# Gate and up by seven products of halves: two of four weight sums of a block moved from VectorE to accumulating DMAs

## Chip, cores and metric

One Trainium2 chip, one core. The metric is device time in microseconds (us) of one execution; lower is better. A chip of its own ran the kernel before three times; differences of about one per cent, 6 us, can be told from none.

## The reference, cut to what matters

A two-layer decoder trunk on 256 tokens of width 1024 in float32. Layer 0 mixes tokens with gated linear attention, layer 1 with block attention; each mixer is followed by a residual layer norm, a SwiGLU FFN of 2816 hidden columns, and another residual layer norm. The change lies in the FFN:

```python
def swiglu_ffn(x, w_gu, w_down):
    gate, up = jnp.split(x @ w_gu, 2, axis=-1)
    return (jax.nn.silu(gate) * up) @ w_down
...
for i in range(DEPTH):
    ...
    x = layer_norm(DEEPNORM_ALPHA * x + y, ln_g[i, 0], ln_b[i, 0])
    x = layer_norm(DEEPNORM_ALPHA * x + swiglu_ffn(x, ffn_w_gu[i], ffn_w_down[i]), ln_g[i, 1], ln_b[i, 1])
```

## The kernel before

**Precision.** Every float32 operand of a matmul is split into a high and a low part (float32r): ScalarE casts the high part (L513 for the units below), VectorE subtracts it from the raw tile to get the low part (L514). A product is then three matmuls on TensorE: high x high, low x high, high x low (`mm3`, L289 to L291; in the blocks below L536, L538, L539).

**The FFN.** `ffn` (L456) first makes 512 of the 2816 columns in the ordinary way (`act_block`), then 2048 columns in four blocks of 512 (`seven`, L523), then the last 256 (tiles g8, u8). In a block the weights of gate and up are seen as four quarters: two halves of the 1024 input rows (kh = 0, 1) by gate and up (gu = 0, 1). A quarter is loaded as two units of 128 x 1024 floats, 512 KB each (`load_unit`, L506, issued on SP's DMA queue). The block's 2 x 2 product of halves (two token halves by two input halves, against the quarters) is done in seven products in place of eight, in the manner of Strassen and Winograd. The left sides are halves of x and four sums of them, made once a layer (`x_sums`, s1 to s4). The right sides are three quarters as they are and four sums of quarters. Each product is 12 matmuls of 128 x 128 by 512 columns, accumulated in the PSUM tiles pa, pb, pc. In program order, with the letter that the trace gives the split units:

- A: quarter (0,0), loaded into the two tiles called A.
- B: A + (0,1), summed in place of A by VectorE (`add_to`, L554 to L556); (0,1) is one of the X tiles.
- C: (1,0), another X pair.
- D: A + (1,1), in place of A, by VectorE.
- E: (1,1), an X pair.
- F: (1,1) + (0,1), in place of the (1,1) pair, by VectorE (L586).
- G: A + (1,0), in place of A, by VectorE (L591).

So a block has eight sums of 128 x 1024 on VectorE (four sums of two units), all recorded at L556, and 14 splits. Silu of gate, the multiplication by up, two sets of transposes (tr, L304) and their split follow; the down projection (fy) of the block before is spread over the block, four rows of w_down at a time (`down_now`, each row loaded and split as d0, d1, ...).

**The order.** Nothing is issued in program order. `Plan` (L64) takes every step with a duration that is written by hand for each engine (`pe`, `act`, `dve`, `gps`, `dma`, L230 to L250) and places the steps one by one, the earliest start first, with 41 SBUF tiles of 128 x 1024 floats (S), two of x (T) and eight PSUM banks to share out. Its result is the order of each engine's queue; on the chip each queue runs in that order and waits on semaphores. `pe` plans columns / 2400 + 0.01 us. `dma_add` (L247) plans a DMA that accumulates, issued on GpSimd's queue: 1.3 us of GpSimd and 4.0 us more until it has landed; the kernel before doesn't call it. GpSimd does little else: some sets of zeros and ones, products of the first mixer, and the small powers of the norms.

The lines that make and use the last two sums:

```python
add_to(r4, 0, 1)
product(pa, "s3", [split_unit(f"F{q}", r4[q]) for q in range(2)], False, False)
...
down_now(pend[2:])
add_to(ch, 1, 0)
product(pa, "a11", [split_unit(f"G{q}", ch[q]) for q in range(2)], False, True)
```

Of the kernel before, what the change touches and what calls it, by code (L numbers as in the profile page):

```python
# [12 lines left out]
ALU = mybir.AluOpType  # L13
# [176 lines left out]
def kernel(ctx, tc, x, positions, gla_w_in, gla_w_gk, gla_b_gk, gla_norm_g, gla_w_out,  # L190
                      moba_w_in, moba_w_out, ffn_w_gu, ffn_w_down, ln_g, ln_b,
                      c_f32, c_i32, out):
    nc = tc.nc
# [16 lines left out]
    pl = Plan(slots)  # L210
# [31 lines left out]
        return pl.op("POOL", 0.2 + 0.0022 * n, fn, reads, writes, **kw)  # L242

    def pe(cols, fn, reads, writes, **kw):
        return pl.op("PE", cols / 2400.0 + 0.01, fn, reads, writes, **kw)

    def dma_add(fn, reads, writes, **kw):  # L247
        return pl.op("POOL", 1.3, fn, reads, writes, extra=4.0, **kw)


    def split(name, parts, zero=False):
# [79 lines left out]
    def Tk(T, t, k):  # L331
        return [(T, ("h", t, k // 4)), (T, ("l", t, k // 4))]
# [64 lines left out]
    def feat_block(banks, T, ws):  # L397
        for i, (wh, wl) in enumerate(ws):
            for hp in range(2):
                def f(i=i, wh=wh, wl=wl, hp=hp):  # L400
                    wv = [w.r.rearrange("p (j c) -> p j c", j=2) for w in (wh, wl)]
                    for hh in range(2):
                        ps = banks[hp].f[:, hh * S:(hh + 1) * S].rearrange("p (t c) -> p t c", t=2)
                        for j in range(2):
                            k = 2 * i + j
                            cs = slice((2 * hp + hh) * P, (2 * hp + hh + 1) * P)
                            mm3(ps, wv[0][:, j, cs], wv[1][:, j, cs], T.ap[0][:, :, k, :], T.ap[1][:, :, k, :],
                                k == 0 and hh == 0, k == KT - 1 and hh == 1)
                pe(12 * 256, f, Tk(T, 0, 2 * i) + Tk(T, 1, 2 * i) + [wh, wl], [banks[hp]])

    def v_block(blk, t, T, ws, vt):
        ps = pl.buf("acc", f"v{blk}{t}")
# [43 lines left out]
    def ffn(i, xs, T, gb, dstT, last, x32):  # L456
# [42 lines left out]
        def unit(kh, gu, q, c0):  # L499
            k0 = 4 * kh + 2 * q  # L500
            return wgu[k0 * P:(k0 + 2) * P, HID * gu + c0:HID * gu + c0 + 512].rearrange("(k p) c -> p k c", p=P)

        def uv(b):
            return b.f.rearrange("p (k c) -> p k c", k=2)

        def load_unit(name, src):  # L506
            raw = S_(name)
            dma(lambda: nc.sync.dma_start(uv(raw), src), 512, [], [raw])
            return raw
# [13 lines left out]
        def seven(b, c0, pend):  # L523


            pa, pc, pb = pl.buf("ps", "pa"), pl.buf("ps", "pc"), pl.buf("ps", "pb")
            e1, e2 = S_("e1"), S_("e2")

            def product(ps, left, ws, first, last_):
                st, rd = lhs(left)  # L530
                for q, (wh, wl) in enumerate(ws):
                    def f(q=q, wh=wh, wl=wl):
                        for j in range(2):
                            sh, sl_ = st(2 * q + j)
                            cs = slice(512 * j, 512 * j + 512)
                            nc.tensor.matmul(ps.f, sh, wh.r[:, cs], start=first and q == 0 and j == 0, stop=False,  # L536
                                             skip_group_check=True)
                            nc.tensor.matmul(ps.f, sl_, wh.r[:, cs], start=False, stop=False, skip_group_check=True)  # L538
                            nc.tensor.matmul(ps.f, sh, wl.r[:, cs], start=False, stop=last_ and q == 1 and j == 1,  # L539
                                             skip_group_check=True)  # L540
                    pe(6 * 512, f, rd + [wh, wl], [ps])

            def keep_(ps, dst, j):
                sl = slice(512 * j, 512 * j + 512)
                act(512, lambda: nc.scalar.copy(dst.f[:, sl], ps.f), [ps], [(dst, j)])  # L545

            have = {}

            def get(kh, gu):
                if (kh, gu) not in have:  # L550
                    have[kh, gu] = [load_unit(f"X{q}", unit(kh, gu, q, c0)) for q in range(2)]
                return have[kh, gu]

            def add_to(raws, kh, gu):  # L554
                for q, other in enumerate(get(kh, gu)):
                    dve(1024, lambda q=q, other=other: nc.vector.tensor_tensor(  # L556
                        out=raws[q].f, in0=raws[q].f, in1=other.f, op=ALU.add), [raws[q], other], [raws[q]])

            ch = [load_unit(f"A{q}", unit(0, 0, q, c0)) for q in range(2)]
            product(pa, "a00", [split_unit(f"A{q}", ch[q]) for q in range(2)], True, False)  # L560
            keep_(pa, e1, 0)
            add_to(ch, 0, 1)
            product(pc, "s1", [split_unit(f"B{q}", ch[q]) for q in range(2)], True, False)
            keep_(pc, e2, 0)
            r3 = get(1, 0)
            product(pb, "a01", [split_unit(f"C{q}", r3[q]) for q in range(2)], True, True)
            dve(512, lambda: nc.vector.tensor_tensor(out=e1.f[:, 0:512], in0=pb.f, in1=e1.f[:, 0:512], op=ALU.add),
                [pb, (e1, 0)], [(e1, 0)])
            act(512, lambda: nc.scalar.activation(e1.f[:, 0:512], e1.f[:, 0:512], AF.Silu), [(e1, 0)], [(e1, 0)],
                table="silu")  # L570
            add_to(ch, 1, 1)
            product(pa, "s2", [split_unit(f"D{q}", ch[q]) for q in range(2)], False, False)
            keep_(pa, e1, 1)
            r4 = get(1, 1)
            down_now(pend[:2])
            product(pc, "s4", [split_unit(f"E{q}", r4[q]) for q in range(2)], False, True)
            h, l = S_(f"hT{b}h", True), S_(f"hT{b}l", True)

            def dst(i, cs):
                return (h, l)[i].r.rearrange("p (k c) -> p k c", k=4)[:, :, cs]  # L580
            dve(512, lambda: nc.vector.tensor_tensor(out=e1.f[:, 512:1024], in0=pc.f, in1=e1.f[:, 512:1024],  # L581
                                                     op=ALU.subtract), [pc, (e1, 1)], [(e1, 1)])
            dve(512, lambda: nc.vector.tensor_tensor(out=e1.f[:, 0:512], in0=e1.f[:, 0:512], in1=e1.f[:, 512:1024],
                                                     op=ALU.mult), [(e1, 0), (e1, 1)], [(e1, 0)])
            transpose_split(e1, (h, l), 0, 0, skey=0, dkey=0, dstf=lambda i: dst(i, slice(0, P)))
            add_to(r4, 0, 1)  # L586
            product(pa, "s3", [split_unit(f"F{q}", r4[q]) for q in range(2)], False, False)
            dve(512, lambda: nc.vector.tensor_tensor(out=e2.f[:, 0:512], in0=e2.f[:, 0:512], in1=pa.f,
                                                     op=ALU.subtract), [pa, (e2, 0)], [(e2, 0)])
            down_now(pend[2:])  # L590
            add_to(ch, 1, 0)  # L591
            product(pa, "a11", [split_unit(f"G{q}", ch[q]) for q in range(2)], False, True)
            act(512, lambda: nc.scalar.activation(e2.f[:, 512:1024], pa.f, AF.Silu), [pa], [(e2, 1)], table="silu")  # L593
            dve(512, lambda: nc.vector.tensor_tensor(out=e2.f[:, 512:1024], in0=e2.f[:, 512:1024], in1=e2.f[:, 0:512],  # L594
                                                     op=ALU.mult), [(e2, 0), (e2, 1)], [(e2, 1)])
            transpose_split(e2, (h, l), 1, 1, skey=1, dkey=1, dstf=lambda i: dst(i, slice(P, 2 * P)))
            return [(c0 // P + j, (h, l), lambda j=j: (hv(h)[:, j, :], hv(l)[:, j, :])) for j in range(4)]
# [3 lines left out]
        for b in (8,):  # L601
            c0 = 512 + 256 * b
# [4 lines left out]
            for q in range(2):  # L607
                for c in range(2):
                    for gi, w2 in ((0, g2), (1, u2)):
                        def f(c=c, q=q, gi=gi, w2=w2, pss=pss):  # L610
                            ps = pss[c].f[:, gi * S:(gi + 1) * S].rearrange("p (t c) -> p t c", t=2)
                            cc = slice(c * P, (c + 1) * P)
                            wv = [w.r.rearrange("p (j c) -> p j c", j=4) for w in w2[q]]
                            for j in range(4):
                                k = 4 * q + j
                                mm3(ps, wv[0][:, j, cc], wv[1][:, j, cc], T.ap[0][:, :, k, :], T.ap[1][:, :, k, :],
                                    k == 0 and gi == 0, k == KT - 1 and gi == 1)
                        pe(12 * 256, f, Tk(T, 0, 4 * q) + Tk(T, 1, 4 * q) + list(w2[q]), [pss[c]])
            for c in range(2):
                ps, sil = pss[c], S_("sil")  # L620
                act(256, lambda ps=ps, sil=sil: nc.scalar.activation(sil.f[:, 0:S], ps.f[:, 0:S], AF.Silu),
# [473 lines left out]
```

## Time and profile before

| | us |
|---|---|
| median of 3 runs | 604.07 (600.82 to 606.42) |
| the profiled execution | 606.1, its span 604.3 |
| TensorE matmuls busy | 580.7 (96% of the span) |
| TensorE weight loads busy | 489.9 (81%) |
| VectorE busy | 525.5 (87%) |
| ScalarE busy | 339.6 (56%) |
| GpSimd busy | 22.2 (4%) |
| 16 DMA engines, mean busy share | 55.5%, 110.02 MB moved |

The times of a profile are those of one profiled execution; its span runs from the first to the last instruction. PE is TensorE's matmuls, PEld its weight loads, which run beside the matmuls; DVE is VectorE, ACT ScalarE, POOL GpSimd, SPq the DMA issues of SyncE. Matmuls are pipelined and their ends are modelled, so a busy TensorE can still be waiting. PEclk is the clock granted to TensorE as a share of full speed: 1.00 is 2.4 GHz, 0.50 is 1.2 GHz. The DMA share is the mean busy share of the 16 DMA engines. "out<-in" names what an instruction writes and reads, in the program's names without buffer numbers.

### The profile page before, as it was taken

Reading aid. Unit: us, or ns where it says so; the run is one execution under the profiler, and the core shown is the slowest. Engines: PE = TensorE matmul, PEld = TensorE weight load, DVE = VectorE, ACT = ScalarE, POOL = GpSimd, SP = SyncE. Lnnn points to the kernel's source line nnn. Section 1 sums busy time; section 2 is a strip of 40 time slices with the busy share of each in tenths; the row PEclk is TensorE's granted clock in tenths of the full one; section 3 lists DMA queues with packets and bytes.
Section 4 is the critical chain, followed back from the end, with each engine's and each line's share of the span. In section 5 each row is a group of like instructions: output and inputs, shape, how many; then the busy total and the mean of one; then the engine's idle time right before and its main releaser. Section 6 shows DMA issues by size and latency. Waiting matters only on the chain.

```text
span 604.3 us, 7959 instructions
## 1 busy us (share of the span) xinstructions
PE 580.7 (96%) x3006; PEld 489.9 (81%) x3006; DVE 525.5 (87%) x643; ACT 339.6 (56%) x452; POOL 22.2 (4%) x27
## 2 busy tenths in 40 slices
PE   8999998999999989899999999999999998998995
PEld 7899886888888668589889999888888885867883
DVE  5888369899999998989898688989999999899956
ACT  4893365357675665676264365735676655567510
POOL 1020210100000000000000000000000000000001
PEclk9999999999999989999999999999999998999998
DMA  8984284544838446476557446535475563836301
GB/s 276 378 280 146 98 284 137 181 142 146 295 113 268 136 146 217 146 264 214 170 178 235 146 149 211 164 85 194 143 244 206 173 237 113 253 116 208 121 0 69
DMA packets 51879, 110.02 MB, mean 182 GB/s; under 512 B 4689, under 2 KB 9329, under 8 KB 51842
## 3 DMA queue, kind: packets, MB, share of 16 engines
q1 hardware_dynamic: 51842, 109.53, 55.5%
q8 instruction: 23, 0.38, 0.3%
q14 instruction: 14, 0.11, 0.1%
HBM read 108.47 MB, written 1.05 MB: 181 GB/s over the span
## 4 chain that ended last, share of the span: by engine, by line
PE 87%; DVE 7%; ACT 2%; DMA 2%; issue 1%; SPq 0%; DVEq 0%
PE fy L289 7%; PE fy L291 7%; PE fy L290 7%; PE pa L539 5%; PE pa L538 5%; PE pa L536 5%; PE v L291 2%; PE v L289 2%; PE v L290 2%; PE tr L304 2%; PE y L291 2%; PE y L289 2%; PE y L290 2%; PE pc L536 2%; PE pc L539 2%; PE pc L538 2%
## 5 line engine op out<-in xcount | busy, mean ns | idle before, releaser
L556 DVE TENSOR_TENSOR A<-A,X 128x1024 f32<-128x1024 f32 x48 | 57.3, 1219 | 0.0
L313 ACT CAST xT<-tr 128x512 fp32r<-128x512 f32 x16 | 9.2, 593 | 40.6 <-PE tr L304 40.4
L360 POOL TENSOR_TENSOR st<-st,mhalf 128x1 f32<-128x1 f32 x8 | 7.5, 944 | 496.3 <-DVE st L358 496.3
L545 ACT COPY e<-pa 128x512 f32<-128x512 f32 x16 | 9.4, 587 | 17.5 <-PE pa L539 17.4
L556 DVE TENSOR_TENSOR X<-X,X 128x1024 f32<-128x1024 f32 x16 | 18.8, 1219 | 0.0
L317 DVE TENSOR_TENSOR xT<-tr,xT 128x512 fp32r<-128x512 f32 x16 | 10.7, 687 | 7.2 <-ACT xT L313 4.6
L513 ACT CAST C0h<-X 128x1024 fp32r<-128x1024 f32 x8 | 8.4, 1050 | 15.0 <-DMA X<-in_ffn_w_gu 15.0
L348 DVE SCALAR_TENSOR_TENSOR r<-xn,fy 128x512 f32<-128x512 f32 x8 | 5.5, 684 | 8.4 <-PE fy L291 8.4
L304 PE MATMUL tr<-ident,e 128*128 128x128 f32 x64 | 9.8, 276 | 3.0 <-DVE e L594 3.0
L304 PEld LDWEIGHTS tr<-ident,e 128*128 128x128 f32 x64 | 7.6, 140 | 6.0 <-DVE e L594 4.7
L352 DVE BATCH_NORM_STATS2 st<-r 128x6 f32<-128x512 f32 x16 | 11.1, 693 | 0.5
L513 ACT CAST G1h<-A 128x1024 fp32r<-128x1024 f32 x8 | 8.4, 1050 | 5.3 <-DVE A L556 5.1
L539 PE MATMUL pa<-D0l,s2hl 128*128 128x512 f32 x16 | 7.3, 455 | 4.2 <-DVE D0l L514 4.2
L370 DVE SCALAR_TENSOR_TENSOR xn<-r,st,lnb 128x512 f32<-128x512 f32 x16 | 11.3, 746 | 0.0
L366 DVE SCALAR_TENSOR_TENSOR r<-r,st,lng 128x512 f32<-128x512 f32 x16 | 11.2, 745 | 0.0
L513 ACT CAST A0h<-A 128x1024 fp32r<-128x1024 f32 x8 | 8.4, 1051 | 5.0 <-DMA A<-in_ffn_w_gu 5.0
L513 ACT CAST F0h<-X 128x1024 fp32r<-128x1024 f32 x8 | 8.4, 1054 | 4.5 <-DVE X L556 4.5
L581 DVE TENSOR_TENSOR e<-pc,e 128x512 f32<-128x512 f32 x8 | 5.5, 691 | 6.2 <-PE pc L539 6.2
L513 ACT CAST C1h<-X 128x1024 fp32r<-128x1024 f32 x8 | 8.4, 1052 | 4.1 <-DMA X<-in_ffn_w_gu 4.1
L513 ACT CAST D0h<-A 128x1024 fp32r<-128x1024 f32 x8 | 8.4, 1048 | 4.1 <-DVE A L556 4.1
L513 ACT CAST G0h<-A 128x1024 fp32r<-128x1024 f32 x8 | 8.4, 1053 | 3.8 <-DVE A L556 3.8
L593 ACT ACTIVATE e<-pa 128x512 f32<-128x512 f32 x8 | 4.8, 595 | 9.3 <-PE pa L539 9.3
(1096 smaller groups left out, 2288.9 us busy)
## 6 DMA issues: line engine op xcount, KB each, us to landing
X<-in_ffn_w_gu SPq DMA_DIRECT2D x48, 512.0 KB, 4.9
A<-in_ffn_w_gu SPq DMA_DIRECT2D x16, 512.0 KB, 3.9
lng<-in_ln_g SPq DMA_DIRECT2D x4, 512.0 KB, 3.6
lnb<-in_ln_b SPq DMA_DIRECT2D x4, 512.0 KB, 5.5
x<-in_x SPq DMA_DIRECT2D x4, 256.0 KB, 4.2
d0r<-in_ffn_w_down SPq DMA_DIRECT2D x2, 512.0 KB, 4.5
d1r<-in_ffn_w_down SPq DMA_DIRECT2D x2, 512.0 KB, 4.9
d2r<-in_ffn_w_down SPq DMA_DIRECT2D x2, 512.0 KB, 3.2
```

Source lines behind the costliest of these rows:

```text
L289: nc.tensor.matmul(ps, lh, rh, start=start, stop=False)
L290: nc.tensor.matmul(ps, ll, rh, start=False, stop=False)
L291: nc.tensor.matmul(ps, lh, rl, start=False, stop=stop)
L304: nc.tensor.transpose(ps.f[:, j * P:(j + 1) * P], src.f[:, k * P:(k + 1) * P], ident.f)
L352: nc.vector.bn_stats(st.f[:, 6 * hf:6 * hf + 6], r.f[:, sl])
L366: nc.vector.scalar_tensor_tensor(out=r.f[:, sl], in0=r.f[:, sl], scalar=st.f[:, 12:13], in1=g.f[:, sl], op0=ALU.subtract, op1=ALU.mult)
L370: nc.vector.scalar_tensor_tensor(out=xn.f[:, sl], in0=r.f[:, sl], scalar=st.f[:, 15:16], in1=b.f[:, sl], op0=ALU.mult, op1=ALU.add)
L513: act(1024, lambda: nc.scalar.copy(hi.r, raw.f), [raw], [hi])
L536: nc.tensor.matmul(ps.f, sh, wh.r[:, cs], start=first and q == 0 and j == 0, stop=False, skip_group_check=True)
L538: nc.tensor.matmul(ps.f, sl_, wh.r[:, cs], start=False, stop=False, skip_group_check=True)
L539: nc.tensor.matmul(ps.f, sh, wl.r[:, cs], start=False, stop=last_ and q == 1 and j == 1, skip_group_check=True)
L556: dve(1024, lambda q=q, other=other: nc.vector.tensor_tensor(out=raws[q].f, in0=raws[q].f, in1=other.f, op=ALU.add), [raws[q], other], [ra ...
```

## The change

VectorE makes only the sums for B and D. The sum for F is now made in the pair (0,1): two DMAs on GpSimd's queue (`add_dma`) read (1,1) from HBM and add it onto the tiles, after the sum for B has read them. The sum for G is made in A: two such DMAs read (1,0) from HBM and add it onto A, after D's split has read A. The three products and all else of a block stay. Three of the planner's numbers change with it: a matmul is planned by columns / 2250, twelve matmuls of 256 columns count as 270 columns each, and an accumulating DMA lands 8.0 us after its issue in place of 4.0.

```diff
     def pe(cols, fn, reads, writes, **kw):
-        return pl.op("PE", cols / 2400.0 + 0.01, fn, reads, writes, **kw)
+        return pl.op("PE", cols / 2250.0 + 0.01, fn, reads, writes, **kw)
 
     def dma_add(fn, reads, writes, **kw):
-        return pl.op("POOL", 1.3, fn, reads, writes, extra=4.0, **kw)
+        return pl.op("POOL", 1.3, fn, reads, writes, extra=8.0, **kw)
...
-                pe(12 * 256, f, Tk(T, 0, 2 * i) + Tk(T, 1, 2 * i) + [wh, wl], [banks[hp]])
+                pe(12 * 270, f, Tk(T, 0, 2 * i) + Tk(T, 1, 2 * i) + [wh, wl], [banks[hp]])
...
+            def add_dma(raws, kh, gu):
+                for q in range(2):
+                    def f(q=q):
+                        nc.gpsimd.dma_start(uv(raws[q]), unit(kh, gu, q, c0), accum_op=ALU.add)
+                    dma_add(f, [raws[q]], [raws[q]])
+
             ch = [load_unit(f"A{q}", unit(0, 0, q, c0)) for q in range(2)]
             product(pa, "a00", [split_unit(f"A{q}", ch[q]) for q in range(2)], True, False)
             keep_(pa, e1, 0)
             add_to(ch, 0, 1)
             product(pc, "s1", [split_unit(f"B{q}", ch[q]) for q in range(2)], True, False)
             keep_(pc, e2, 0)
+            add_dma(get(0, 1), 1, 1)
             r3 = get(1, 0)
             product(pb, "a01", [split_unit(f"C{q}", r3[q]) for q in range(2)], True, True)
...
             add_to(ch, 1, 1)
             product(pa, "s2", [split_unit(f"D{q}", ch[q]) for q in range(2)], False, False)
             keep_(pa, e1, 1)
+            add_dma(ch, 1, 0)
             r4 = get(1, 1)
             down_now(pend[:2])
             product(pc, "s4", [split_unit(f"E{q}", r4[q]) for q in range(2)], False, True)
...
-            add_to(r4, 0, 1)
-            product(pa, "s3", [split_unit(f"F{q}", r4[q]) for q in range(2)], False, False)
+            product(pa, "s3", [split_unit(f"F{q}", have[0, 1][q]) for q in range(2)], False, False)
...
             down_now(pend[2:])
-            add_to(ch, 1, 0)
             product(pa, "a11", [split_unit(f"G{q}", ch[q]) for q in range(2)], False, True)
...
-                        pe(12 * 256, f, Tk(T, 0, 4 * q) + Tk(T, 1, 4 * q) + list(w2[q]), [pss[c]])
+                        pe(12 * 270, f, Tk(T, 0, 4 * q) + Tk(T, 1, 4 * q) + list(w2[q]), [pss[c]])
```

## Rows read from the trace of the kernel before

**Rows 1.** Stretches: length, busy PE, PEld, DVE, ACT, POOL (instructions), clock, DMA share, GB/s.

```profile
176.79:207.30 30.51, 29.53 (x136) 24.05 (x134) 28.89 (x30) 20.25 (x24) 0.00 (x0) 1.00 0.66 207
207.30:244.33 37.03, 34.05 (x143) 26.22 (x142) 34.07 (x34) 21.55 (x26) 0.00 (x0) 0.95 0.53 171
244.33:281.86 37.53, 35.50 (x169) 28.72 (x168) 35.31 (x35) 24.39 (x28) 0.00 (x0) 0.95 0.65 210
...
500.60:536.87 36.27, 34.08 (x143) 26.34 (x142) 34.04 (x34) 21.06 (x26) 0.00 (x0) 0.95 0.55 174
...
sum 273.16, PE 261.63 PEld 210.37 DVE 257.89 ACT 174.70 POOL 0.00; mean PE 32.70 PEld 26.30 DVE 32.24 ACT 21.84 POOL 0.00
```

**Rows 2.** Chain that ended last, around 204 to 218 us: start us, us, what.

```profile
204.09 0.23 PE pa L538
...
212.29 2.27 DVE A L556 x2
...
217.63 0.43 PE pa L539
```

**Rows 3.** Waits of TensorE's matmuls: waiter <- releaser, us in total, times, longest.

```profile
PE pa L539 <- DVE D0l L514: 4.2, 4, 1.1
PE tr L304 <- DVE e L594: 3.0, 4, 1.0
PE pc L539 <- DVE B1l L514: 2.1, 4, 0.9
PE pa L536 <- ACT D0h L513: 2.1, 4, 0.5
```

**Rows 4.** Waits of TensorE's weight loads.

```profile
PEld pa L539 <- DVE D0l L514: 6.0, 4, 1.5
PEld tr L304 <- DVE e L594: 4.7, 4, 1.4
PEld pc L539 <- DVE B1l L514: 3.8, 4, 1.3
PEld pa L536 <- ACT D0h L513: 3.8, 4, 1.0
...
PEld pc L539 <- DVE B0l L514: 1.9, 4, 0.6
```

**Rows 5.** Timeline of TensorE in the third block: start us, us, instruction [idle before <-releaser].

```profile
214.91 0.39 PE L538 MATMUL pa<-D0h,s2hl 128*128 128x512 f32 x1
...
216.35 0.50 PE L539 MATMUL pa<-D0l,s2hl 128*128 128x512 f32 x1 [1.05 <-DVE D0l L514]
```

**Rows 6.** Costliest groups of instructions, L556: busy us, mean ns of one | idle before.

```profile
L556 DVE TENSOR_TENSOR A<-A,X 128x1024 f32<-128x1024 f32 x48 | 57.3, 1219 | 0.0
...
L556 DVE TENSOR_TENSOR X<-X,X 128x1024 f32<-128x1024 f32 x16 | 18.8, 1219 | 0.0
```

**Rows 7.** Timeline of VectorE in the third block.

```profile
203.87 2.35 DVE L556 TENSOR_TENSOR A<-A,X 128x1024 f32<-128x1024 f32 x2
...
216.21 1.22 DVE L514 TENSOR_TENSOR D1l<-A,D1h 128x1024 fp32r<-128x1024 f32 x1
...
221.89 2.36 DVE L556 TENSOR_TENSOR X<-X,X 128x1024 f32<-128x1024 f32 x2
...
235.24 1.22 DVE L556 TENSOR_TENSOR A<-A,X 128x1024 f32<-128x1024 f32 x1
```

**Rows 8.** Timeline of ScalarE in the third block.

```profile
223.14 1.05 ACT L513 CAST F0h<-X 128x1024 fp32r<-128x1024 f32 x1 [1.08 <-DVE X L556]
...
231.68 1.06 ACT L513 CAST C0h<-X 128x1024 fp32r<-128x1024 f32 x1 [5.58 <-DMA X<-in_ffn_w_gu]
...
234.49 1.06 ACT L513 CAST G0h<-A 128x1024 fp32r<-128x1024 f32 x1
```

**Rows 9.** The page: GB/s that the DMA engines moved, span in 40 slices.

```profile
GB/s 276 378 280 146 98 284 137 181 142 146 295 113 268 136 146 217 146 264 214 170 178 235 146 149 211 164 85 194 143 244 206 173 237 113 253 116 208 121 0 69
```

**Rows 10.** The page: DMA issues of the X units: count, KB each, median us to landing.

```profile
X<-in_ffn_w_gu SPq DMA_DIRECT2D x48, 512.0 KB, 4.9
```

## The prediction, made before the changed kernel ran

> **What bounds the kernel now.** I read the busy time by stretch first, then the chain that ended last, the waits of TensorE, and the timeline around one of those waits. The part that the change touches is eight blocks of 512 FFN columns, four in each layer. I cut the trace where a block's first product of a sum starts. Over the eight stretches, 273.16 us, VectorE is busy 32.24 us of each block's mean 34.15 [rows 1]. Two stretches differ: the second block takes 30.51 us, the third 37.03 us with seven more matmul records, worth 7 x 0.23 = 1.6 us at the step that a matmul of 512 columns takes when nothing holds it [rows 1, 2]. So the third block loses some 5 us, and in it VectorE is busy 34.07 us, longer than the whole second block. VectorE falls behind TensorE a little in every block; in blocks three and four the lead is used up.
>
> The chain says the same: after 204.3 us it leaves TensorE, runs through ScalarE and VectorE (two sums of 2.27 us among them), and comes back to TensorE at 216 us, with matmuls of 0.43 us instead of 0.23 [rows 2, 5]. TensorE's waits name four places, each met four times: the transposes of the block before (behind e, L594), B1l, D0h and D0l. By the matmuls' own idle time they cost 11.4 us [rows 3]; by the idle time of the weight loads, with B0l as a fifth place, 20.2 us [rows 4]. The first is too low, since a matmul's end is modelled late; the second too high, since a load normally runs ahead of its matmul. One case can be read off: the matmul on D0l starts 1.44 us after the one before it, where 0.23 is usual, so 1.21 us are lost [rows 5]. I take the middle of the two sums, 15.8 us.
>
> Then the clock. After the idle places the granted clock fell to the lower of its two levels: three of the four late stretches show a mean of 0.95, the second block 1.00 [rows 1]. 5% of some 37 us is 1.8 us in each, 5 us in all; the matmuls of 0.43 us are these [rows 2]. Together 21 us of 606.1 (the profiled execution's own time) are lost because VectorE is late. The rest of a block is TensorE at its own pace: (273.16 - 21) / 8 = 31.5 us a block.
>
> **The change part by part.** *Sums taken from VectorE.* 64 sums of 1.22 us stand on L556, eight a block [rows 6]; back to back, a pair takes 2.36 us, so each costs 1.15 [rows 7]. Four a block go: 4 x 1.15 = 4.6 us, and VectorE's share falls from 32.24 to 27.6 us, 3.9 us under TensorE's 31.5. The sums that go are those of the block's second half (the F sum at 221.89 us, the second G sum at 235.24), where TensorE did not wait. But VectorE's queue is one line: what stands behind them (the splits of A, the s1 sums, B, C, the D sums) moves forward by up to 4.6 us, against about 4 us lost in a block's waits. The two pairs that stay are those on the chain. So I expect these waits to go but for small ones, 0.25 us a block, 2 us in all; and the low clock with them, as it came only after such idle time.
>
> *Sums given to DMAs.* Four transfers of 512 KB a block, issued by GpSimd, which is busy 0.00 us in all these stretches [rows 1]; whatever their issue takes there is hidden. No such transfer is in the trace. What they need of the 16 DMA engines I bound by a load. The second block moves 207 GB/s x 30.51 us = 6.3 MB, twelve loads, at a DMA share of 0.66: 20.1 us of all engines, 1.68 us a load [rows 1]. That share contains waiting; at the most that any fortieth of the span moved, 378 GB/s, a load takes 1.39 us [rows 9]. An accumulating transfer moves the source once and touches the destination twice. Not below a load, then (1x: no byte less than a load moves); 2x if the extra read takes as long as the transfer itself; 3x if all three passes come one after another. I take 2x, the case nearest to bytes moved. A block then needs of the DMA engines, at 1.39 and at 1.68 us: 1x 22.2 to 26.9 us; 2x 27.8 to 33.6; 3x 33.4 to 40.3; TensorE needs 31.5. At 2x, with a middle of 30.7, the engines are nearly full but not the bound. Loads will land later than the 4.9 us they take now [rows 10], and ScalarE, in order, already stood 5.58 us before the cast of a late C0 [rows 8]; behind it wait the casts of hT and G0. For this crowding I take 0.5 us a block, 4 us in all; the ends are 0 and the rival below.
>
> The Trainium skill, page "Collectives: The Full Stack", section "The bandwidth ceiling: the fold count and why AG ≠ RS ≠ AR", says that an add inside a DMA posts two read descriptors on the same ring and ran 1.93 times as long as a copy there. With 1.93 in place of 2 a block would need 27.4 to 33.1 us of the engines (an estimate by that page); no run here shows it yet.
>
> *Are the sums in time?* VectorE has read X (the second gate/up half) when the s1 pair ends, 206.2 us, and F0's cast starts at 223.14: 16.9 us. The D split has read A at 217.4, G0's cast starts at 234.49: 17.1 us [rows 7, 8]. With blocks shorter by up to 5.5 us, 11 to 12 us remain. A pair at 2x takes 2 x 2 x 1.39 to 1.68 = 5.6 to 6.7 us of full engines plus the landing; sharing them with loads, about 10. It fits, without much room.
>
> *Buffers and waits.* The X that held the third half is free after the C split, not after the G sum; the one that becomes the F sum is held through the block as before. The casts of F and G, which wait for VectorE's sums today, will wait for a DMA; behind them on ScalarE stand the next casts and the Silu.
>
> *The planner's numbers.* A matmul of 512 columns is now planned at 0.23 us (512/2250), the measured step [rows 2]; before it was 0.21. This reorders queues in the whole program and adds no instruction. Outside the FFN blocks TensorE shows few long waits, so I take 0, between a gain of 3 and a loss of 5 us.
>
> Sum: 606.1 - 21 + 2 + 4 = 591.1 us for an execution like the profiled one; that one ran 2.0 us above the median of the runs, 604.07. So 589 us.
>
> **The rivals.** *Crowded engines.* At 2x and 1.68 us a load the engines need 33.6 us, 2.1 more than TensorE: 8 x 2.1 = 17 us come back. 606.1 - 21 + 2 + 17 - 2 = 602 us; between this and my sum, 596 to 602. For it: the share of 0.66 already, and loads that come late now. Against it: 378 GB/s were reached.
>
> *The accumulating transfers become the bound (slower).* At 3x the need is 33.4 to 40.3 us, middle 36.9: 8 x 5.4 = 43 us, 606.1 - 21 + 2 + 43 - 2 = 628 us, TensorE waiting for F0h and G0h. It decides where a block needs more than the 34.15 us of today: over 2.1x by the slow rate, over 3.1x by the fast one. Against it: both destinations have 17 us.
>
> *GpSimd cannot write the transfers' descriptors while VectorE works.* VectorE is idle 2.96 us of the third block's 37.03 [rows 1], a gap of 1 us every 12 us or so. If an issue waited for such a gap, 6 us on the average came on top of a pair's 10, 4.5 us more than the 11.5 of room: for one pair of each block 8 x 4.5 = 36 us, 589 + 36 = 625 us. Nothing in the trace speaks for it, and nothing against it, GpSimd being idle there. The Trainium skill, page "SBUF — State Buffer", section "Who interferes with whom", says that the two share a port pair, held by the faster copies of VectorE; it infers that sums of two tensors leave descriptor writing alone. By that rule this rival falls.
>
> **How the numbers follow.** My forecast, 579 to 596 us: 0.62. Crowded engines, 596 to 604: 0.18. Transfers as the bound: 0.14. Descriptors held up: 0.06. The best case is all 21 us and the 3 of the planner: 604.07 - 24 = 580, less a little for the spread of runs. To hold 8 in 10 the range is 578 to 607 us; the likeliest case alone is 579 to 596. One per cent, about what a measurement of this kernel can tell from none, is 6 us: faster is below 598, slower above 610. Faster: the forecast's 0.62 and a third of the crowded case, 0.68. Same: the other 0.12 and 0.04 of the last two, 0.16. Slower: 0.16.
>
> **What would show it.** Right: L556 with 32 sums; third and fourth blocks near 31.5 us with the clock at 1.00; no waits of TensorE on B1l or D0l; VectorE under 28 us a block with gaps; the DMA share in the blocks from 0.66 to 0.85 or more. Wrong: waits of TensorE on F0h or G0h, ScalarE standing long for A or X, a DMA share near 1 with blocks over 33 us, or long issues on GpSimd while VectorE works.

## The result and the profile after

The changed kernel took 622.29 us (618.37 to 625.03); the kernel before, on the same chip, 602.62. The ratio is 1.031, its 95% interval 1.023 to 1.040: slower, by some 3%, 19 us. Forecast were 589 us and a range of 578 to 607. The profiled execution took 625.03 us, its span 623.3.

The page of the kernel after: DMA share in 40 slices and the two DMA queues (packets, MB, share of 16 engines), the group of L556 and the two groups of the new line, and the landing of the issues from both queues (KB each, median us).

```profile
DMA  8975184449989798888365545625898998878301
...
q1 hardware_dynamic: 51842, 109.53, 52.5%
q0 software_dynamic: 8704, 16.78, 15.7%
...
L556 DVE TENSOR_TENSOR A<-A,X 128x1024 f32<-128x1024 f32 x32 | 38.2, 1218 | 6.4 <-DMA X<-in_ffn_w_gu 6.4
...
L562 POOL DMA_DIRECT2D X<-in_ffn_w_gu x16 | 19.6, 1239 | 127.8 <-DVE A L556 48.9
...
L562 POOL DMA_DIRECT2D A<-in_ffn_w_gu x16 | 19.2, 1202 | 95.4 <-DVE D0l L514 67.6
...
X<-in_ffn_w_gu SPq DMA_DIRECT2D x48, 512.0 KB, 5.1
...
X<-in_ffn_w_gu POOLq DMA_DIRECT2D x16, 512.0 KB, 9.4
A<-in_ffn_w_gu POOLq DMA_DIRECT2D x16, 512.0 KB, 8.3
```

The change did what it says: 32 sums are left on VectorE in place of 64 [rows 6], and 32 transfers stand on GpSimd's queue, 1.2 us of GpSimd each. The DMA engines are nearly full in the FFN blocks, a share of 0.83 to 0.94 in the stretches below. By the shares of the two queues, one accumulating transfer took 15.7% x 623.3 / 32 = 3.06 us of all sixteen engines; a load of SP's took 52.5% x 623.3 us / 109.53 MB x 0.524 MB = 1.57 us. That is 1.95 times. In the median an X unit landed hardly later than before, 5.1 us after its issue in place of 4.9 [rows 10]; what hurts are those that land much later, as the chain below shows.

Three stretches of the first layer's blocks, cut as before the change from one B product to the next (columns as in [rows 1]):

```profile
149.72:182.78 33.06, 30.70 (x139) 25.17 (x138) 27.84 (x28) 20.92 (x25) 5.99 (x5) 1.00 0.94 259
182.78:221.02 38.24, 32.19 (x146) 26.00 (x144) 34.53 (x34) 25.99 (x31) 6.03 (x5) 0.99 0.89 229
221.02:257.48 36.46, 32.39 (x143) 26.25 (x141) 29.54 (x30) 21.18 (x26) 4.85 (x4) 0.97 0.83 228
```

VectorE has gaps now, 29.54 us busy of 36.46, yet the blocks are as long as the late ones before. What TensorE waits for has moved. Its waits (us in total, times, longest) name no B1l and no D0l any more [rows 3], but the transposes, behind e:

```profile
PE tr L304 <- DVE e L600: 16.0, 6, 4.4
...
PE tr L304 <- DVE e L591: 9.0, 6, 3.4
```

And e is late because the queues ahead of it stood before a load. The chain that ended last, in the third block (start us, us, what):

```profile
242.57 9.19 DMA d12r<-in_ffn_w_down
251.78 1.06 ACT d12h L261
...
255.15 1.12 DVE E0l L514
256.28 0.70 DVE e L600
257.02 0.71 PE tr L304 x4
```

A row of w_down, d12, took 9.2 us to land. Its first product ran only at 267.3 us, but its cast stands in ScalarE's queue, and ScalarE takes its queue in order: what stood behind d12h came late, E0l, e, the transposes, TensorE. That load is the last of a row of delays, not all of it. ScalarE's timeline, with one line of VectorE's in the middle (start us, us, instruction, idle before and what ended it):

```profile
244.92 1.05 ACT L513 CAST C1h<-X 128x1024 fp32r<-128x1024 f32 x1 [3.89 <-DMA X<-in_ffn_w_gu]
...
248.89 1.23 DVE L556 TENSOR_TENSOR A<-A,X 128x1024 f32<-128x1024 f32 x1 [0.58 <-DMA X<-in_ffn_w_gu]
...
251.78 1.05 ACT L261 CAST d12h<-d12r 128x1024 fp32r<-128x1024 f32 x1 [0.52 <-DMA d12r<-in_ffn_w_down]
```

For d12 itself ScalarE stood idle only 0.52 us. It had stood 3.89 us before C1h for a late X unit, and the D sum behind it waited for another X unit.

### The profile page after: what moved, and what is told of

Its sections match the earlier page's. It is cut to its first block, busy times and chain, and to the rows that moved or that the text cites. A ratio compares the mean times of both kernels' runs of the same rounds, so it can differ in the third digit from the quotient of the medians.

```text
span 623.3 us, 8115 instructions
## 1 busy us (share of the span) xinstructions
PE 583.9 (94%) x3006; PEld 493.7 (79%) x3006; DVE 493.2 (79%) x611; ACT 339.0 (54%) x452; POOL 61.1 (10%) x59
## 3 DMA queue, kind: packets, MB, share of 16 engines
q1 hardware_dynamic: 51842, 109.53, 52.5%
q0 software_dynamic: 8704, 16.78, 15.7%
## 4 chain that ended last, share of the span: by engine, by line
PE 39%; DMA 14%; DVE 11%; issue 5%; ACT 4%; DVEq 0%; ACTq 0%; SPq 0%
DMA d12r<-in_ffn_w_down 3%; PE fy L289 3%; PE fy L290 3%; PE fy L291 3%; DMA d7r<-in_ffn_w_down 2%; PE tr L304 2%; DVE A L556 2%; DMA X<-in_ffn_w_gu 2%; DMA A<-in_ffn_w_gu 1%; DMA d15r<-in_ffn_w_down 1%; PE mk L291 1%; PE mq L291 1%; PE mq L289 1%; PE mk L289 1%; PE mk L290 1%
## 5 line engine op out<-in xcount | busy, mean ns | idle before, releaser
L556 DVE TENSOR_TENSOR A<-A,X 128x1024 f32<-128x1024 f32 x32 | 38.2, 1218 | 6.4 <-DMA X<-in_ffn_w_gu 6.4
L562 POOL DMA_DIRECT2D X<-in_ffn_w_gu x16 | 19.6, 1239 | 127.8 <-DVE A L556 48.9
L562 POOL DMA_DIRECT2D A<-in_ffn_w_gu x16 | 19.2, 1202 | 95.4 <-DVE D0l L514 67.6
L513 ACT CAST B0h<-A 128x1024 fp32r<-128x1024 f32 x8 | 8.4, 1052 | 17.1 <-DVE A L556 17.1
L348 DVE SCALAR_TENSOR_TENSOR r<-xn,fy 128x512 f32<-128x512 f32 x8 | 5.5, 685 | 11.3 <-PE fy L291 11.2
L514 DVE TENSOR_TENSOR D1l<-A,D1h 128x1024 fp32r<-128x1024 f32 x8 | 9.8, 1222 | 3.6 <-ACT D1h L513 3.6
L370 DVE SCALAR_TENSOR_TENSOR xn<-r,st,lnb 128x512 f32<-128x512 f32 x16 | 11.3, 744 | 0.0
L514 DVE TENSOR_TENSOR A0l<-A,A0h 128x1024 fp32r<-128x1024 f32 x8 | 9.8, 1220 | 1.5 <-ACT A0h L513 1.3
L513 ACT CAST D1h<-A 128x1024 fp32r<-128x1024 f32 x8 | 8.4, 1045 | 4.1 <-PE pa L538 3.0
L514 DVE TENSOR_TENSOR G1l<-A,G1h 128x1024 fp32r<-128x1024 f32 x8 | 9.8, 1219 | 0.4 <-ACT G1h L513 0.4
L514 DVE TENSOR_TENSOR G0l<-A,G0h 128x1024 fp32r<-128x1024 f32 x8 | 9.7, 1217 | 0.2 <-ACT G0h L513 0.2
L514 DVE TENSOR_TENSOR B0l<-A,B0h 128x1024 fp32r<-128x1024 f32 x8 | 9.8, 1219 | 0.1
```

The source lines that it names most:

```text
L370: nc.vector.scalar_tensor_tensor(out=xn.f[:, sl], in0=r.f[:, sl], scalar=st.f[:, 15:16], in1=b.f[:, sl], op0=ALU.mult, op1=ALU.add)
L513: act(1024, lambda: nc.scalar.copy(hi.r, raw.f), [raw], [hi])
L514: dve(1024, lambda: nc.vector.tensor_tensor(out=lo.r, in0=raw.f, in1=hi.f, op=ALU.subtract), [raw, hi], [lo])
L556: dve(1024, lambda q=q, other=other: nc.vector.tensor_tensor(out=raws[q].f, in0=raws[q].f, in1=other.f, op=ALU.add), [raws[q], other], [ra ...
L562: nc.gpsimd.dma_start(uv(raws[q]), unit(kh, gu, q, c0), accum_op=ALU.add)
```

## The experiments

Three things changed at once: who makes the sums, what the DMA engines carry, and the order of every queue, since the planner got new numbers. The theory after reading the trace ("crowding"): transfers of two loads' length fill the engines, loads land late, and queues in a fixed order pass the delay on. The rivals: the new order alone costs; or the F and G sums themselves land late. All ratios are against the kernel before on the same chip (603.9 to 604.9 us).

**The planner's numbers alone** (e1): the kernel before with these two edits.

```diff
-        return pl.op("PE", cols / 2400.0 + 0.01, fn, reads, writes, **kw)
+        return pl.op("PE", cols / 2250.0 + 0.01, fn, reads, writes, **kw)
...
-                pe(12 * 256, f, ...)
+                pe(12 * 270, f, ...)
```

> The kernel before with only the planner's two TensorE numbers changed (columns / 2250, twelve matmuls of 256 columns as 270 each); all sums stay on VectorE. Crowding theory (the accumulating transfers hold the DMA engines 2.1 times as long as loads, loads land late, ScalarE and VectorE stand in line behind them): 600 to 606 us, as before. Planner theory (the new order of the queues is what costs): 612 us or more. Both in part: 606 to 610 us, the 5 us by which the changed kernel is late already when its first FFN starts, where no sum has moved yet.

Measured: 594.91 us, ratio 0.984 (0.978 to 0.989). No theory had said that it would be faster. The stretches show what the new order does, from the second block's B on:

```profile
177.15:208.40 31.25, 31.09 (x143) 25.48 (x141) 31.25 (x32) 21.56 (x25) 0.00 (x0) 1.00 0.62 214
208.40:240.65 32.25, 32.25 (x149) 26.68 (x147) 32.25 (x33) 20.29 (x25) 0.00 (x0) 1.00 0.59 200
```

VectorE is busy without a gap, 32.25 of 32.25 us; before it had 3 us of gaps in a block of 37 [rows 1]. The order, not VectorE's work alone, had made the late blocks 37 us long.

**The accumulating DMAs with the planner's old numbers** (e2): the changed kernel with both edits above taken back.

> The changed kernel with TensorE's numbers of the planner as before (columns / 2400, 256), the accumulating DMAs kept. Crowding theory: 612 to 620 us, the loss stays. Planner theory: 585 to 598 us, the gain that was forecast appears.

Measured: 613.09 us, 1.012 (1.007 to 1.018). So the new numbers cost the changed kernel 9.2 us (by the two ratios, each against its own chip, nearer 12) and give the kernel before 9.0; and the adds cost 9.2 us without them. Neither alone is the answer.

**Plain loads in place of the adds** (e3), and **an eighth of each add** (e4). Both have, instruction by instruction, the queue order of the changed kernel on TensorE, VectorE, ScalarE and SP.

```diff
-                        nc.gpsimd.dma_start(uv(raws[q]), unit(kh, gu, q, c0), accum_op=ALU.add)
+                        nc.gpsimd.dma_start(uv(raws[q]), unit(kh, gu, q, c0))
```

```diff
-                        nc.gpsimd.dma_start(uv(raws[q]), unit(kh, gu, q, c0), accum_op=ALU.add)
+                        nc.gpsimd.dma_start(uv(raws[q])[:, :, 0:64], unit(kh, gu, q, c0)[:, :, 0:64],
+                                            accum_op=ALU.add)
```

> The changed kernel with the 32 accumulating DMAs made plain loads of the same bytes from the same queue: same order of every queue, but no add (the F and G products use the quarter that was loaded, not the sum). Crowding theory: packets of 84 in place of 176 ns, about half of the engines' extra work gone, 600 to 612 us. Planner or order theory: 618 to 625 us, as the order is unchanged.

> The changed kernel with each accumulating DMA cut to 64 of 512 columns (an eighth of the bytes), same number of issues and the same order of every queue; the other columns of the F and G sums are left out. Crowding theory: the DMA share in the blocks falls back to 0.7, TensorE's waits mostly go, 585 to 600 us. Planner or order theory: 615 us or more, as the order, the buffers and the issues on GpSimd are unchanged.

Measured: 605.79 us (1.000, 0.997 to 1.004) and 592.08 us (0.979, 0.974 to 0.983). In one and the same order the time follows what the transfers take of the engines. (They also land sooner, after 5.0 to 6.1 us in e3 in place of 8.3 to 9.4; e5 and e6 take that apart.) By the share of GpSimd's queue in the page's third part, one transfer takes 3.06 us of all engines (622.3 us), a plain one 8.4% x 605.2 / 32 = 1.59 us (605.8 us), an eighth 4.0% x 591.4 / 32 = 0.74 us (592.1 us). The rival "order alone" falls: in that very order, with an eighth of the bytes, the kernel is 30 us faster than the changed one and 12 us below the kernel before. Crowding was right within its numbers.

The row of e3 (packets, MB, share):

```profile
q0 software_dynamic: 4608, 16.78, 8.4%
```

**More loads that nobody reads** (e5, e6): the kernel of e1, all sums on VectorE, with four or eight plain loads more in a block, from GpSimd into a spare tile, each group behind a one-column copy that waits for the B sum or D's split.

```diff
+            def more_loads(after, kh, gu, slots):
+                g = pl.buf("m", "gate")
+                pl.op("POOL", 0.3, lambda: nc.gpsimd.tensor_copy(g.f[:, 0:1], after.f[:, 0:1]), [after], [g])
+                for s_ in slots:
+                    ...
+                        nc.gpsimd.dma_start(dst.rearrange("p (k c) -> p k c", k=2), unit(kh, gu, s_ % 2, c0))
+                    dma_add(f, [g], [(spare, s_)])
```

> Planner's numbers alone (594.9 us) with all sums on VectorE, and four plain loads of 512 KB more in each block, from GpSimd's queue into a spare tile that nothing reads, at the places where the changed kernel adds (two after the B sum, two after D's split). If the loads' share of the DMA engines is what costs: 602 to 610 us, as with plain loads in place of the adds. If what costs is that the F and G sums themselves land late: 594 to 597 us, as these sums stay on VectorE.

> As the one before with eight more plain loads a block, about the time on the DMA engines of four accumulating transfers (8 x 84 against 4 x 176 ns a packet). Share theory: 615 to 625 us, the changed kernel's time without a single accumulating DMA. Late-sum theory: 594 to 598 us.

Measured: 598.21 us (0.991, 0.988 to 0.995) and 614.77 us (1.019, 1.016 to 1.022), against 594.91 without the loads; the queues of TensorE, VectorE, ScalarE and SP are in the same order in all three. The copies that hold the groups back cost little: ScalarE waited for them 3.2 us in all in e5 and 2.9 in e6. Eight loads cost 20 us though not one sum depends on a DMA: late sums are not the cause, or not the main one. Four cost 3 us, less than expected: the price is not in proportion to the traffic.

**Only the G sum by DMA** (e8): `add_dma(get(0, 1), 1, 1)` taken out, the F sum made by `add_to(r4, 0, 1)` as before.

> The changed kernel with only the G sum made by accumulating DMAs (two a block), the F sum back on VectorE: half the added traffic. Share theory: 602 to 611 us, half-way between the planner's numbers alone and the changed kernel. If it is the number of GpSimd waits or the F sum that costs: near 595 us.

Measured, in a queue order of its own: 597.54 us, 0.990 (0.986 to 0.993): lower than the share theory said, in line with the four loads of e5. The first half of the traffic costs little, the second half 25 us.

**Loads planned late** (e7, and again with five rounds, e12): the changed kernel, full transfers, with one number of the planner changed.

```diff
     def dma(fn, kb, reads=(), writes=(), **kw):
-        return pl.op("SP", kb / 360.0, fn, reads, writes, extra=2.3, **kw)
+        return pl.op("SP", kb / 360.0, fn, reads, writes, extra=6.0, **kw)
```

> The changed kernel, all four sums as it has them, with the planner told that a plain load lands 6.0 us after its transfer time in place of 2.3. If the loss comes from queues that were ordered for loads that land early (casts of late tiles stand ahead of work that is ready): 598 to 612 us. If the engines are simply too full to feed TensorE: 617 to 627 us, unchanged or worse.

> The changed kernel with loads planned at 6.0 us once more, beside the version with all sums on VectorE and the same planner's numbers, in five rounds: 589 to 595 us. If moving the sums helps: 3 us or more below the version on VectorE; if not, within 2 us of it.

Measured: 591.87 us (0.982, 0.978 to 0.986) and 591.95 us (0.977, 0.974 to 0.980). The whole loss is gone, with the same transfers, which hold the engines for 16.7% of the span (e12; 15.7% in the changed kernel). So the loss takes two things: transfers that crowd the engines, and an order that believes a load of 512 KB is there 3.7 us after its issue (512 / 360 + 2.3).

**The same number without the DMA sums** (e9: e1 with 6.0; e11: the kernel before with 6.0), and **with the eight spare loads** (e10: e6 with 6.0).

> All eight sums of a block on VectorE, the planner with the new TensorE numbers and loads planned to land after 6.0 us: the changed kernel with loads at 6.0 us, but without its accumulating DMAs. If taking two sums from VectorE is worth something once the queues are ordered for late loads: 594 to 600 us, slower than the version with the adds. If VectorE was not the bound, only the order: 589 to 593 us, the same or faster.

> The kernel before with loads planned at 6.0 us and nothing else changed (TensorE's old numbers, all sums on VectorE). If the planned landing of loads is what orders the queues well, whatever the sums: 590 to 600 us. If TensorE's number was what the kernel before lacked: 600 to 606 us, as before.

> The kernel with eight more plain loads a block (614.8 us), its planner told that loads land after 6.0 us. Order theory (full DMA engines cost only where the queues were ordered for early loads): 592 to 602 us. If full engines cost by themselves: 610 us or more.

Measured: e9 592.89 us (0.979, 0.976 to 0.983), e11 601.57 us (0.993, 0.991 to 0.996), e10 604.22 us (0.999, 0.995 to 1.002). The number by itself is worth 2 to 3 us. With the new TensorE numbers, the sums on DMAs (591.95) and on VectorE (592.89) cannot be told apart. e10 is between the two theories: of the 20 us that the spare loads cost, 11 stay. In that kernel VectorE still has all the sums and is busy in 247.9 of its blocks' 255.5 us, so it has little room to make up for a late load; whether that is why, no run shows.

**An eighth of each add, in the two other orders** (e13: e2 cut as e4; e14: e7 cut as e4).

> The changed kernel with TensorE's old planner numbers and each accumulating DMA cut to an eighth of its bytes (the other columns of the F and G sums are left out): the kernel before with four sums a block taken from VectorE at almost no price. If VectorE's load was the bound in the old order, as the prediction had it: 583 to 592 us, some 15 us or more below the kernel before. If it was only the order: 598 to 606 us.

> The changed kernel with loads planned at 6.0 us and each accumulating DMA cut to an eighth (the other columns of the F and G sums are left out): what the full transfers still cost in that order. If the order takes all of their cost away: 590 to 593 us, as with full transfers (591.9). If some is left: 584 to 589 us.

Measured: e13 585.75 us, 0.966 (0.961 to 0.971); e14 587.69 us, 0.970 (0.966 to 0.974). e13 takes the sums from VectorE at little price with TensorE's old numbers, and the time falls by 19.1 us. It is not the order of the kernel before, though: without the sums the planner places all queues anew. By e14, the full transfers still cost 4 us where loads are planned at 6.0 (587.69 against 591.95 in e12). In e13 the waits on VectorE went; in six stretches TensorE is busy throughout, as in this one:

```profile
208.65:239.52 30.87, 30.87 (x143) 25.55 (x141) 29.71 (x30) 21.23 (x26) 4.85 (x4) 1.00 0.70 212
```

**Full adds, old TensorE numbers, loads at 6.0** (e15: e2 with 6.0), the cell that was missing.

> The full accumulating DMAs, TensorE's old planner numbers, loads planned at 6.0 us: the cell that is missing between 613.1 us (old numbers, loads at 2.3) and 591.9 us (new numbers, loads at 6.0). If the planned landing of loads does it whatever TensorE's numbers: 586 to 595 us. If both numbers are needed: 600 us or more.

Measured: 582.33 us, 0.964 (0.960 to 0.968): the fastest, 22 us below the kernel before, with every sum made. First e2: one block's stretch, then waits of TensorE and of ScalarE.

```profile
179.31:213.69 34.38, 31.06 (x143) 25.48 (x141) 29.21 (x30) 21.44 (x26) 4.79 (x4) 1.00 0.88 245
```

```profile
PE tr L304 <- DVE e L591: 19.2, 8, 3.3
...
ACT A0h L513 <- DMA A<-in_ffn_w_gu: 14.3, 7, 2.7
ACT A1h L513 <- DMA A<-in_ffn_w_gu: 12.1, 8, 3.5
```

The same of e15, and from its page the DMA share in 40 slices and the landing of SP's X units.

```profile
173.04:203.91 30.87, 30.87 (x143) 25.55 (x141) 29.71 (x30) 20.64 (x25) 4.82 (x4) 1.00 0.99 276
```

```profile
PE tr L304 <- DMA x<-in_x: 0.6, 1, 0.6
...
ACT A1h L513 <- DMA A<-in_ffn_w_gu: 9.4, 5, 3.2
...
ACT A0h L513 <- DMA A<-in_ffn_w_gu: 4.9, 3, 2.4
```

```profile
DMA  8994175549999998996366435526799999999101
...
X<-in_ffn_w_gu SPq DMA_DIRECT2D x48, 512.0 KB, 7.1
```

In e2 each of six stretches loses 1.4 to 3.3 us, once a block, at the transposes behind e (L591). In e15 TensorE waits for nothing in the blocks, 30.87 of 30.87 us, while the engines carry 276 GB/s at a share of 0.99, more than in e2 (0.88). Its loads land no sooner: its X units after 7.1 us in the median, against 6.3 in e2 and 5.1 in the changed kernel. ScalarE still waits for late tiles; as TensorE has no waits, nothing that it needs soon can stand behind them. How such a delay travels, from the chain of e2, second block, and behind it ScalarE's cast and TensorE's transpose with the idle time before them:

```profile
184.91 10.28 DMA A<-in_ffn_w_gu
...
195.26 0.23 ACT A1h L513
...
198.43 1.22 DVE A1l L514
199.65 1.14 DVE G1l L514
200.79 0.60 DVE e L589
201.39 1.13 DVE A L556
202.52 0.61 DVE e L591
...
203.27 0.63 PE tr L304 x4
```

```profile
195.26 1.05 ACT L513 CAST A1h<-A 128x1024 fp32r<-128x1024 f32 x1 [2.83 <-DMA A<-in_ffn_w_gu]
...
203.27 0.63 PE L304 MATMUL tr<-ident,e 128*128 128x128 f32 x4 [3.32 <-DVE e L591]
```

A1 landed after 10.3 us. Its cast and low part are work for the next block (A1h's first product ran at 211.9 us), but G0, G1 and e stand behind them in the queues, and TensorE waited 3.32 us for e.

All cells, medians in us (the kernel before took 602.6 to 604.9 on the chips used):

| TensorE numbers, loads planned | all sums on VectorE | an eighth of each add | full adds |
|---|---|---|---|
| old, 2.3 | 604.07 (before) | 585.75 (e13) | 613.09 (e2) |
| old, 6.0 | 601.57 (e11) | | 582.33 (e15) |
| new, 2.3 | 594.91 (e1) | 592.08 (e4) | 622.29 (after) |
| new, 6.0 | 592.89 (e9) | 587.69 (e14) | 591.95 (e12) |

## Why the prediction was wrong

**VectorE as the bound, and what taking the sums is worth: right in size, right in mechanism only in part.** The sum had -21 + 2 = -19 us; e13 measured 604.8 - 585.75 = 19.1 us, and its stretches have TensorE busy throughout, the clock at 1.00. But e13 has another order than the kernel before, and order alone is worth much of this. The four blocks of the first layer, from the first B product to the first product of the last 256 columns, in the kernel before, e1, e13 and the changed kernel (columns as in [rows 1]):

```profile
144.32:275.57 131.25, 125.26 (x541) 99.90 (x540) 123.05 (x121) 85.87 (x100) 0.00 (x0) 0.97 0.60 196
...
146.22:270.91 124.69, 122.85 (x547) 100.61 (x546) 123.63 (x122) 84.94 (x99) 0.00 (x0) 0.99 0.62 208
...
146.86:267.28 120.42, 120.42 (x548) 99.69 (x547) 115.38 (x114) 86.17 (x101) 16.86 (x14) 1.00 0.75 228
...
149.67:287.47 137.80, 124.90 (x547) 101.49 (x546) 116.03 (x113) 87.41 (x102) 16.86 (x14) 0.98 0.88 245
```

With the second layer (129.84, 123.48, 121.40 and 137.20 us) the blocks take 261.1, 248.2, 241.8 and 275.0 us. Of the 19.3 us between the kernel before and e13, the order of e1 wins 12.9 with every sum still on VectorE, which then is busy 123.63 of 124.69 us; the other 6.4 are left for the sums and for what the order of e13 adds. What was read as VectorE's load was for the greater part VectorE's gaps, and an order made them. With the new TensorE numbers the same sums were worth 2.8 us (e1 to e4) and 5.2 (e9 to e14). That the sum came out at 19 is luck in part. Two smaller readings were off. The 31.5 us a block are too long, since the fourth stretches ran 6.3 us past their blocks, with 26 more matmul records than the third [rows 1]: over the blocks alone it is (261.1 - 21) / 8 = 30.0 us, and e13 took 241.8 / 8 = 30.2. And VectorE's busy time fell from 525.5 to 493.2 us, 1.0 us a sum in place of 1.15; per block it did not fall under 28 us, as other work moved up. In the first layer's blocks of the changed kernel it is 116.03 / 4 = 29.0; 16 sums left them, but VectorE's instructions there fell only from 121 to 113.

**The price of a transfer on the engines: right.** 2x was taken, 1.95x measured (3.06 to 1.57 us), and it agrees with the Trainium skill, page "Collectives: The Full Stack", section "The bandwidth ceiling: the fold count and why AG ≠ RS ≠ AR", by which an add inside a DMA ran 1.93 times as long as a copy. The share in the blocks was to be 0.85 or more; it was 0.83 to 0.94 in the stretches above.

**The crowding: the step that failed.** From "nearly full but not the bound" I took 0.5 us a block, 4 us in all. Measured in one order, an eighth against the full adds: 613.09 - 585.75 = 27.3 us with the old TensorE numbers, 622.29 - 592.08 = 30.2 with the new. The argument compared what the engines need in a block with what TensorE needs, and so asked for capacity. Capacity was not short: e15 moves the same bytes at a share of 0.99 and TensorE doesn't wait. What was short was the time that the order allowed a load: 3.7 us planned, 4.9 us in the median before [rows 10], and 9.2 and 10.3 us for the late ones on the chains under the crowd. The row that should have told was there: ScalarE stood 5.58 us before C0 [rows 8]. The prediction even names what waits behind that cast, hT and G0, and still takes half a microsecond a block; it was a sample of what every cast of a late load does to the queue behind it. The rival named for this, crowded engines, had the place right and the mechanism wrong, and 602 us as its price was 20 us low. Not all of the loss lies in the blocks: of the 19.0 us by which the changed kernel's span is longer, 13.9 do, but 5.4 stand before the first B product (149.67 against 144.32 us), where no sum has moved. e4, with the same order and an eighth of each add, gets there at 148.3 us, so most of the 5.4 belong to the order.

**The planner's numbers: the second step that failed.** They were taken at 0, between a gain of 3 and a loss of 5 us. They win 9.0 us where VectorE makes all sums (e1) and lose 6.3 to 9.6 us in the three pairs with DMA sums (e13 to e4, e2 to after, e15 to e12). A truer duration of one engine is not a better order while another engine's is wrong. Why the sign turns with the sums is not settled.

By medians, then: -19.1 for the sums (with the order that goes with them), +27.3 for the crowding in an order planned for early loads, +9.2 for the new TensorE numbers. These are steps from cell to cell, so they add up to the difference by construction, and another path divides it otherwise: with the new numbers first it is -9.0, then -2.8 for the sums, then +30.2 for the crowding.

**The other rivals.** Transfers as the bound: the need of 3x did not come, and e15 speaks against it. Descriptors held up by VectorE: an issue took 1.20 us of GpSimd (L562) in the changed kernel, and e15 lost nothing by it with VectorE busy 95% of its six stretches. That agrees with the Trainium skill, page "SBUF — State Buffer", section "Who interferes with whom", which infers that sums of two tensors leave descriptor writing alone. The sums' room was judged rightly: landing in 8.3 to 9.4 us, against 11 to 12, and TensorE's waits in the changed kernel name neither F nor G. Of the signs of being wrong, ScalarE standing long for A or X came (3.89 us before C1h), with blocks of 33 to 38 us, but the waits of TensorE on F0h or G0h did not.

**What stays open.** Which of the many moves in e15's order matter was not taken apart: the planner reorders all queues at once, and only two landing times, 2.3 and 6.0, were tried. e10's remaining 11 us are unexplained, too.

## What to carry to other kernels

When work is moved to the DMA engines, ask not only whether the engines have room for the bytes but how late every other load becomes, and what stands behind its first reader in an in-order queue. A planned order carries the old landing time in it, so the traffic and the planned landing are changed together: here that one number, 2.3 to 6.0 us, was worth 30 us. A planner's numbers are tried one at a time, since a truer duration for one engine won 9 us in one version of this kernel and cost 9 in another.

## What the hardware showed that was not expected

The sixteen DMA engines ran at a share of 0.95 to 0.99 through whole FFN blocks, 266 to 276 GB/s with adds among the loads, and TensorE lost no time by it (e15). The price of traffic grew in a step, not a line: four more loads a block cost 3.3 us and eight cost 19.9 (e5, e6, in one queue order). An add of an eighth of the bytes took a quarter of the engines' time, 0.74 of 3.06 us. And in e10 a GpSimd copy of a single column took from 0.18 to 11.3 us beside a busy VectorE, where GpSimd's DMA issues took 0.73 on the average; what held the copies is not shown. The longer of the two groups (shortest, median and longest in ns), and the issues:

```profile
L562 POOL COPY gate<-D1l x8: 178/645/11257, 148.4 to 545.4; 128x1 f32<-128x1 f32 x8
...
L566 POOL DMA_DIRECT2D spare<-in_ffn_w_gu x64 | 46.3, 726 | 11.0 <-DMA spare<-in_ffn_w_gu 10.1
```
